# The last z tile inside attention's first steps: its product split over steps 1, 3, 4 and 5, its reciprocal in eight pieces

## The chip, the cores and the metric

The kernel runs on one core of one Trainium2 chip. The metric is the device time of one execution in microseconds (us), and a kernel's time is the median of several executions.

## The reference

One encoder layer on 1024 tokens of width 1024, in float32. What matters here is the middle of it:

```
u = x @ w_in                                   # -> q | k | v | z | x_ssd | B | C | dt
att_out = softmax(q k^T / 8) v                 # 8 query heads of 64, 2 key/value heads, all 1024 keys
y = ssd(...)                                   # two chunked scans, forward and backward
y = y * silu(z)                                # z: 1024 x 512, silu(z) = z / (1 + exp(-z))
mix = concat(att_out, rms(y) * ssd_norm) @ w_out
```

Ahead of it and behind it stand a SwiGLU block, and at the end a gated embedding, each with a layer norm.

## The kernel before

All large products are made from float32 values that are split in two parts each (a rounded high part and the rest, the low part), so that one product of a 128-row block takes three matmuls: high by low, low by high, high by high (`mm3`, L116 to L122). `lo` (L87) is the VectorE subtraction that makes a low part.

The program runs in stages: first SwiGLU; the z tiles; the q, k, v and convolution products; attention; the scans with the first half of `w_out` between them; the second SwiGLU; the gate. z is computed in eight tiles of 128 tokens. Tiles 0 to 5 are made in `z_part`, tile 6 at the end of `xbc_part`, and tile 7 in `z_last` (L1036), which attention calls.

Attention (L1133) is one loop of 72 steps. There are 16 units (two halves of the queries, four pairs of heads, two heads) of four query tiles each, so 64 query tiles. Step i does, in this order:

- `scores(i)`: four matmuls (L1159) into one of two double PSUM tiles named `big`;
- `turn(i - 2)`: eight 128x128 transposes (L1181) of the probabilities of query tile i - 2, into two PSUM tiles named `sm`, and for each a ScalarE cast (L1183), the high part;
- `values`: from step 6 on, four matmuls (L1196, L1197) with v, a quarter of a unit's sum, which fills one `sm` tile over four steps; after the fourth, L1203 (ScalarE) and L1204 (VectorE) take it out, and after every second unit a small reciprocal `rinv` (L1207);
- `normalise`: every eight steps four transposes (L1218) and a VectorE product (L1219);
- `softmax(i)`: a VectorE maximum over the scores (L1166), then a ScalarE exponential (L1168);
- `begin()` in step 1 alone;
- the two VectorE low parts (L87) of `turn`'s tiles;
- in every even step from 8 on, one entry of the list `aside`.

The pool `sm` has four PSUM tiles, each one bank. Which of them an instruction gets, and the order of the instructions on VectorE, ScalarE, GpSimd and the DMA queue, is set by a scheduler when the program is built. TensorE's instructions keep the written order (`in_order`, L1892). An entry of `aside` is put on VectorE and ScalarE behind what the step has issued there (`behind`, L82).

`begin` (in `run`, L1578) calls `z_last`, issues the loads of four 512 KB blocks of `w_out`, and fills `aside`: first z's seven entries, then four that prepare tables for the scans, then eight that split the `w_out` blocks (a ScalarE cast L108, a GpSimd subtraction L87). z's entries are: add 1 to exp(-z) on GpSimd (L1046), the reciprocal of it on VectorE in four pieces of 128 columns (L1049), and the product with z on GpSimd with its store (L1052, L1053). The store is read in the last stage of the scans (L1411).

Of the kernel before, what the change touches and what calls it, by code (L numbers as in the profile page):

```python
# [12 lines left out]
AF = mybir.ActivationFunctionType  # L13
# [5 lines left out]
P = 128  # L19
S = 1024  # L20
D = 1024
NT = S // P
KD = D // P
# [13 lines left out]
class Layer:  # L37
# [998 lines left out]
    def z_last(self, xT, aside):  # L1036

        nc, V = self.nc, self.nc.vector
        ps = self.z_product(NT - 1, xT)
        r = self.ring.tile([P, 1024], F32, name="blk")  # L1040
        z, e = r[:, :512], r[:, 512:]
        V.tensor_copy(z, ps)
        nc.scalar.activation(out=e, in_=ps, func=AF.Exp, scale=-1.0)

        def one_more():
            nc.gpsimd.tensor_scalar(out=e, in0=e, scalar1=1.0, scalar2=None, op0=ALU.add)  # L1046

        def invert(m):
            V.reciprocal(e[:, m], e[:, m])  # L1049

        def silu():
            nc.gpsimd.tensor_tensor(out=z, in0=z, in1=e, op=ALU.mult)  # L1052
            nc.sync.dma_start(out=self.zd[NT - 1], in_=z)  # L1053
        aside += [one_more, *(lambda m=slice(i * P, (i + 1) * P): invert(m) for i in range(4)), silu]


    def ssd_prep(self, wk):
# [75 lines left out]
    def attention(self, c, mixT, aside, begin):  # L1133

        nc, tc = self.nc, self.tc
        Q, K, V = self.qkv
# [6 lines left out]
        def scores(i):  # L1143
            qh, hp, hh = units[i // 4]
            qt, h = i % 4, hp * 2 + hh
            if qt == 0:
                if hh == 0:
                    st[qh, hp] = dict(
                        raw=ev.tile([P, 512], F32, name="a_raw", bufs=2),
                        rsum=self.small.tile([P, 2, 4], F32, name="rsum"))  # L1150

                st[qh, hp, hh] = [[p.tile([P, 4, 512], F32R, name=n) for n in names] for p, names in (
                    ((pt_pool, ("pth0", "pth1")), (pt_pool, ("ptl0", "ptl1"))),
                    ((self.xp, ("xh01", "xl01")), (self.xp, ("xh11", "xl11"))))[hh]]
            q0 = qh * 512 + qt * P
            ps = self.psb()
            for n in range(2):
                for j in range(2):
                    nc.tensor.matmul(ps[:, n * 512:(n + 1) * 512], lhsT=Q[:, h, q0:q0 + P], rhs=K[:, h // 4, j, n * 512:(n + 1) * 512], start=j == 0, stop=j == 1)  # L1159
            return ps  # L1160

        def softmax(i, ps):
            qh, hp, hh = units[i // 4]
            qt = i % 4
            nm = self.small.tile([P, 1], F32, name="nm")
            nc.vector.tensor_reduce(out=nm, in_=ps, axis=AX.X, op=ALU.max, negate=True)  # L1166
            pr = pp.tile([P, S], F32, name="pr")
            nc.scalar.activation(out=pr, in_=ps, func=AF.Exp, bias=nm, scale=1.0, accum_out=st[qh, hp]["rsum"][:, hh, qt:qt + 1])  # L1168
            st[i] = pr

        def turn(i):
            qh, hp, hh = units[i // 4]
            qt = i % 4
            pth, ptl = st[qh, hp, hh]
            pr = st.pop(i)
            los = []
            for half in range(2):
                pt = self.pss().rearrange("p (k t) -> p k t", t=P)
                for k in range(4):
                    kk = half * 4 + k  # L1180
                    nc.tensor.transpose(out=pt[:, k], in_=pr[:, kk * P:(kk + 1) * P], identity=self.ident)  # L1181
                hi, lo = (x[half][:, :, qt * P:(qt + 1) * P] for x in (pth, ptl))
                nc.scalar.copy(out=hi, in_=pt)  # L1183
                los.append((lo, pt, hi))
            return los

        def values(u, part):
            qh, hp, hh = units[u]
            g = (hp * 2 + hh) // 4
            pth, ptl = st[qh, hp, hh]  # L1190
            if part == 0:
                st["po"] = self.pss()
            po = st["po"]
            for k in (2 * part, 2 * part + 1):
                vw = V[:, k, g].rearrange("p a d -> p (a d)")
                nc.tensor.matmul(po, lhsT=vw, rhs=pth[k // 4][:, k % 4], start=k == 0, stop=False)  # L1196
                nc.tensor.matmul(po, lhsT=vw, rhs=ptl[k // 4][:, k % 4], start=False, stop=k == KD - 1)  # L1197
            if part < 3:
                return
            del st[qh, hp, hh]  # L1200
            raw, rsum = st[qh, hp]["raw"], st[qh, hp]["rsum"]
            mine, other = (slice(j * 64, (j + 1) * 64) for j in (hh, 1 - hh))
            nc.scalar.copy(out=raw[mine], in_=po[other])  # L1203
            nc.vector.tensor_tensor(out=raw[mine], in0=po[mine], in1=raw[mine], op=ALU.add)  # L1204
            if hh:
                rinv = self.small.tile([P, 2, 4], F32, name="rinv")
                nc.vector.reciprocal(rinv, rsum)  # L1207
                rx = ev.tile([P, 4, 2, 64], F32, name="rx")
                nc.gpsimd.tensor_copy(rx, rinv.rearrange("p h q -> p q h").unsqueeze(3).broadcast_to([P, 4, 2, 64]))
                st["norm"] = (qh, hp, rx, raw)  # L1210

        def normalise():
            if "norm" not in st:
                return
            qh, hp, rx, raw = st.pop("norm")
            R = self.pss()
            for qt in range(4):
                nc.tensor.transpose(out=R[:, qt * P:(qt + 1) * P], in_=rx[:, qt].rearrange("p h d -> p (h d)"), identity=self.ident)  # L1218
            nc.vector.tensor_tensor(out=raw, in0=raw, in1=R, op=ALU.mult)  # L1219
            hi, lo = (x[:, hp] for x in mixT[qh][0])  # L1220
            nc.gpsimd.tensor_copy(hi, raw)
            nc.gpsimd.tensor_tensor(out=lo, in0=raw, in1=hi.bitcast(F32), op=ALU.subtract)

        n = 4 * len(units)
        for i in range(n + 8):
            ps = scores(i) if i < n else None
            los = turn(i - 2) if 2 <= i < n + 2 else []
            if 6 <= i < n + 6:
                values((i - 6) // 4, (i - 6) % 4)
            if (i - 6) % 4 == 1:  # L1230
                normalise()
            if ps is not None:
                softmax(i, ps)
            if i == 1:
                begin()
            for a in los:
                self.lo(*a)
            if i >= 8 and i % 2 == 0 and aside:
                with self.behind(mybir.EngineType.Activation), self.behind(mybir.EngineType.DVE):
                    aside.pop(0)()  # L1240
# [292 lines left out]
    def run(self):  # L1533
        nc, tc, I = self.nc, self.tc, self.I
        stop = I.get("_stop", 99)
# [35 lines left out]
        with ExitStack() as c:  # L1571
            self.in_proj(c, xT)
            rctx.close()
            with self.behind(mybir.EngineType.SP):
                tabs = self.ssd_tables(tables)
            blocks0, aside = [], []

            def begin():  # L1578
                self.z_last(xT, aside)
                early = [self.ring_raw(I["wm"][k]) for k in range(4)]  # L1580
                aside.extend(tabs)
                aside.extend(lambda i=i, r=r: blocks0.append(self.split(r[:, i * 512:(i + 1) * 512], eng=nc.gpsimd)) for i in range(2) for r in early)

            mixT = [[self.unit(h, 0)] for h in range(2)]
            with ExitStack() as c2:
                self.attention(c2, mixT, aside, begin)
# [27 lines left out]
        late = sctx.enter_context(tc.tile_pool(name="slate", bufs=2))  # L1614
# [80 lines left out]
        with ExitStack() as xc:  # L1695
# [3 lines left out]
            V = nc.vector  # L1699
# [182 lines left out]
        with ExitStack() as c:  # L1882
            rctx.close()
            acc, xT, wg, tp, turn = self.ffn_y(c, 2, lambda t: y2[t], hS, I["wo2"], wT, [I["wg"][0, k] for k in range(4)], xln=1)
# [98 lines left out]
```

## Time and profile before

| | |
|---|---|
| median of 3 runs | 1947.11 us (1946.96 to 1948.23) |
| the profiled execution: its own time | 1948.74 us |
| the profiled execution: span of the trace | 1946.9 us |
| TensorE clock granted | 0.998 of full speed |
| attention's first score load | 878.37 us into the span |
| first matmul of the scans behind it | 1065.27 us |

The span is the time from the first to the last instruction in the trace. The profile names each instruction by its line, its engine, its operation and the tiles that it writes and reads; PE is TensorE's matmuls, PEld TensorE's weight loads, DVE is VectorE, ACT is ScalarE, POOL is GpSimd. In a row of the timeline the first number is the start in us from the span's start, the second the duration, and brackets at the end tell how long the engine sat idle before it and which instruction ended that. A matmul's end is modelled, so the starts of the weight loads, which stand beside every matmul, show TensorE's pace best.

### The profile page before, as it was taken

The page shows a single profiled execution, that of the slowest core. Times are in us where ns is not written, and L with a number is a line of the kernel's source. Part 1 is how long each engine was busy: PE and PEld are TensorE (multiplying, and loading weights), DVE is VectorE, ACT ScalarE, POOL GpSimd, SP SyncE. Part 2 cuts the span into 40 slices and gives each one's busy share as a digit, 9 for nine tenths or more (in the row PEclk, how much of TensorE's full clock was granted, in tenths as well). Part 3 has the DMA queues.
Part 4 walks back from the last instruction along what each step waited for, and adds up shares of the span by engine and source line. Part 5 has one row for each costly group of instructions (what it writes and reads, how often), then busy time and mean ns, then how long its engine had stood idle before and what let it go on. Part 6 is the DMA issues. An engine that isn't in the chain of part 4 may idle for free.

```text
span 1946.9 us, 25645 instructions
## 1 busy us (share of the span) xinstructions
PE 1927.9 (99%) x9132; PEld 1607.8 (83%) x9132; DVE 1528.0 (78%) x2356; ACT 881.1 (45%) x1509; POOL 416.9 (21%) x310
## 2 busy tenths in 40 slices
PE   8999999999999999999999999999999999999998
PEld 6888888888888889888888888888888888888886
DVE  7977777767678668758998878997787787877698
ACT  6433333325444224537887876633333333443311
POOL 0144535430001032001221001013444440001011
PEclk9999999999999999999999999999999999999999
DMA  8434554549866111231002663244545439976022
GB/s 296 143 125 151 190 179 156 190 159 373 297 221 212 63 42 50 84 119 68 7 1 77 212 222 121 90 165 156 190 163 178 173 121 358 331 262 226 32 77 97
DMA packets 147713, 310.34 MB, mean 159 GB/s; under 512 B 18128, under 2 KB 30800, under 8 KB 147584
## 3 DMA queue, kind: packets, MB, share of 16 engines
q1 hardware_dynamic: 147584, 308.69, 45.4%
q8 instruction: 72, 1.18, 0.2%
q14 instruction: 57, 0.47, 0.1%
HBM read 217.21 MB, written 91.42 MB: 159 GB/s over the span
## 4 chain that ended last, share of the span: by engine, by line
PE 94%; DVE 3%; DMA 1%; ACT 1%; issue 1%; POOL 0%; SPq 0%; DVEq 0%; ACTq 0%
PE sm L122 59%; PE big L516 12%; PE sm L516 9%; PE big L122 3%; PE big L1159 3%; PE sm L1181 2%; PE sm L1196 1%; PE sm L1197 1%; DMA yd<-y 1%; DVE nm L1166 1%; DVE conv L977 1%; PE sm L1270 0%; PE big L224 0%; PE sm L224 0%; PE big L909 0%
## 5 line engine op out<-in xcount | busy, mean ns | idle before, releaser
L122 PE MATMUL sm<-xh,blk 128*128 128x512 f32 x1424 | 439.8, 389 | 0.0
L122 PEld LDWEIGHTS sm<-xh,blk 128*128 128x128 f32 x1424 | 267.3, 188 | 55.4
L122 PE MATMUL sm<-xl,blk 128*128 128x512 f32 x736 | 283.8, 389 | 0.0
L122 PE MATMUL sm<-blk,xl 128*128 128x512 f32 (+2 forms) x784 | 238.2, 371 | 0.2 <-ACT xn_t L1010 0.2
L122 PE MATMUL sm<-blk,xh 128*128 128x512 f32 (+2 forms) x584 | 203.3, 379 | 1.6 <-DVE acc L1466 1.1
L108 ACT CAST blk<-raw 128x512 fp32r<-128x512 f32 (+1 forms) x168 | 101.3, 611 | 215.0 <-PE sm L122 134.1
L87 DVE TENSOR_TENSOR blk<-s,blk 128x512 fp32r<-128x512 f32 x176 | 150.8, 861 | 35.2 <-ACT blk L108 33.2
L87 DVE TENSOR_TENSOR blk<-raw,blk 128x512 fp32r<-128x512 f32 (+1 forms) x168 | 146.5, 875 | 40.6 <-ACT blk L108 40.1
L108 ACT CAST blk<-s 128x512 fp32r<-128x512 f32 x172 | 105.7, 622 | 146.5 <-PE sm L122 118.3
L122 PEld LDWEIGHTS sm<-blk,xl 128*128 128x128 f32 x784 | 142.8, 188 | 24.2 <-ACT xn_t L1010 0.5
L122 PEld LDWEIGHTS sm<-xl,blk 128*128 128x128 f32 x736 | 138.2, 188 | 28.6
L178 POOL TENSOR_TENSOR ln_k<-ln_k,mhalf 128x1 f32<-128x1 f32 x32 | 37.4, 1173 | 579.2 <-DVE ln_k L177 563.0
L516 PE MATMUL big<-xh 128*128 128x512 f32 x576 | 138.8, 390 | 0.0
L267 POOL TENSOR_TENSOR s<-raw 128x512 f32<-128x512 f32 x34 | 55.0, 1617 | 387.2 <-DVE blk L87 381.7
L87 DVE TENSOR_TENSOR xh<-blk,xh 128x1024 fp32r<-128x1024 f32 x78 | 95.4, 1223 | 48.4 <-ACT xh L462 42.3
L462 ACT CAST xl<-blk 128x1024 fp32r<-128x1024 f32 x76 | 80.2, 1055 | 113.5 <-PE sm L516 43.7
L462 ACT CAST xh<-blk 128x1024 fp32r<-128x1024 f32 x78 | 82.3, 1055 | 108.1 <-PE big L516 49.9
L122 PEld LDWEIGHTS sm<-blk,xh 128*128 128x128 f32 x584 | 109.9, 188 | 21.3 <-DVE acc L1466 1.4
L516 PEld LDWEIGHTS big<-xh 128*128 128x128 f32 x576 | 107.8, 188 | 22.2
L87 DVE TENSOR_TENSOR xl<-blk,xl 128x1024 fp32r<-128x1024 f32 x76 | 92.7, 1220 | 41.3 <-ACT xl L462 36.7
L516 PE MATMUL big<-xl 128*128 128x512 f32 x480 | 115.8, 390 | 0.0
L122 PE MATMUL sm<-xET2h,blk 128*128 128x512 f32 x352 | 108.4, 389 | 0.0
(343 smaller groups left out, 4018.5 us busy)
## 6 DMA issues: line engine op xcount, KB each, us to landing
raw<-in_wi_dram SPq DMA_DIRECT2D x81, 512.0 KB
blk<-hS SPq DMA_DIRECT2D x154, 256.0 KB
hS<-h SPq DMA_DIRECT2D x88, 256.0 KB
wr<-in_wo_dram SPq DMA_DIRECT2D x44, 512.0 KB
blk<-wT SPq DMA_DIRECT2D x88, 256.0 KB
hS<-sg SPq DMA_DIRECT2D x66, 256.0 KB
wT<-wr SPq DMA_DIRECT2D x66, 256.0 KB
blk<-in_wo_dram SPq DMA_DIRECT2D x66, 256.0 KB
```

Source lines behind the costliest of these rows:

```text
L87: (eng or self.nc.vector).tensor_tensor(out=out, in0=full, in1=hi.bitcast(F32), op=ALU.subtract)
L108: self.nc.scalar.copy(out=b[:, 0, :n], in_=src)
L122: self.nc.tensor.matmul(ps, lhsT=a, rhs=b, start=(i == 0), stop=(i == n - 1))
L178: nc.gpsimd.tensor_tensor(out=r, in0=v, in1=self.mhalf[:, :1], op=ALU.pow)
L267: lambda: G.tensor_tensor(out=s1, in0=a21, in1=a22, op=ALU.add),
L462: A.copy(out=b[:, :, 0], in_=r)
L516: nc.tensor.matmul(ps[q], lhsT=b[:, 0, x, cut], rhs=b[:, 1, y], start=j == i == 0, stop=j == NP - 1 and i == 2)
L977: nc.vector.scalar_tensor_tensor(out=a[:, o], in0=ps[:, o.start + d - c:o.stop + d - c], scalar=cw[:, j, tap:tap + 1], in1=a[:, o], op0=AL ...
L1159: nc.tensor.matmul(ps[:, n * 512:(n + 1) * 512], lhsT=Q[:, h, q0:q0 + P], rhs=K[:, h // 4, j, n * 512:(n + 1) * 512], start=j == 0, stop=j ...
L1166: nc.vector.tensor_reduce(out=nm, in_=ps, axis=AX.X, op=ALU.max, negate=True)
L1181: nc.tensor.transpose(out=pt[:, k], in_=pr[:, kk * P:(kk + 1) * P], identity=self.ident)
L1196: nc.tensor.matmul(po, lhsT=vw, rhs=pth[k // 4][:, k % 4], start=k == 0, stop=False)
```

## The change

`z_last` no longer makes the whole product of tile 7 in step 1. The 24 matmuls of its eight input blocks are cut into four parts: five blocks (15 matmuls) in step 1, and one block (3 matmuls) in each of the steps 3, 4 and 5, behind that step's softmax. The copy out of PSUM and the exponential follow the last part, in step 5. The reciprocal is made of eight entries of 64 columns in `aside` in place of four of 128, so all entries behind the reciprocals move by four entries, which is eight steps. `attention` gets the three late parts from `begin`.

```diff
     def z_last(self, xT, aside):
 
         nc, V = self.nc, self.nc.vector
-        ps = self.z_product(NT - 1, xT)
+        ps = self.pss()
+        pairs = [(x, (w[:, 0], w[:, 1])) for x, w in zip(self.tok(xT, NT - 1), self.wz)]
+
+        def part(ks):
+            for k in ks:
+                (xh, xl), (wh, wl) = pairs[k]
+                for i, (x, w) in enumerate(((xh, wl), (xl, wh), (xh, wh))):
+                    nc.tensor.matmul(ps, lhsT=x, rhs=w, start=k == i == 0, stop=k == KD - 1 and i == 2)
+        part(range(KD - 3))
         r = self.ring.tile([P, 1024], F32, name="blk")
         z, e = r[:, :512], r[:, 512:]
-        V.tensor_copy(z, ps)
-        nc.scalar.activation(out=e, in_=ps, func=AF.Exp, scale=-1.0)
+
+        def end():
+            part((KD - 1,))
+            V.tensor_copy(z, ps)
+            nc.scalar.activation(out=e, in_=ps, func=AF.Exp, scale=-1.0)
...
-        aside += [one_more, *(lambda m=slice(i * P, (i + 1) * P): invert(m) for i in range(4)), silu]
+        aside += [one_more, *(lambda m=slice(i * 64, (i + 1) * 64): invert(m) for i in range(8)), silu]
+        return [lambda: part((KD - 3,)), lambda: part((KD - 2,)), end]
...
             if i == 1:
-                begin()
+                late = begin()
+            if 3 <= i < 6:
+                late.pop(0)()
```

On TensorE the program read before, from the end of z's product (L122, blocks `blk`) on: L1159 are the scores, L1181 the transposes of the probabilities `pr`.

```order
L122 MATMUL sm<-blk,xh_5609 128x512
L122 MATMUL sm<-blk,xl_5608 128x512
L1159 MATMUL big<-K,Q 128x512 x4
L1181 MATMUL sm<-ident,pr 128x128 x8
L1159 MATMUL big<-K,Q 128x512 x4
L1181 MATMUL sm<-ident,pr 128x128 x8
```

Now it reads there, where z's product is L1046, the scores L1171 and the transposes L1193:

```order
L1046 MATMUL sm<-blk,xl_5608 128x512
L1171 MATMUL big<-K,Q 128x512 x4
L1193 MATMUL sm<-ident,pr 128x128 x8
L1171 MATMUL big<-K,Q 128x512 x4
L1193 MATMUL sm<-ident,pr 128x128 x8
L1046 MATMUL sm<-blk,xl_5608 128x512
L1046 MATMUL sm<-blk,xh_5609 128x512
L1046 MATMUL sm<-blk,xl_5608 128x512
L1171 MATMUL big<-K,Q 128x512 x4
L1193 MATMUL sm<-ident,pr 128x128 x8
```

Nine of z's matmuls moved from step 1 behind the transposes of steps 3, 4 and 5; the first such group is shown.

On VectorE, at the first reciprocals (steps 10 to 12), the program read before (L1166 is the maximum, L1204 the addition behind a unit's last values, L87 the low parts, L1049 z's reciprocal):

```order
L1166 TENSOR_REDUCE nm<-big 128x1
L1204 TENSOR_TENSOR a_raw<-sm,a_raw 64x512
L87 TENSOR_TENSOR ptl_7793<-sm,pth_7791 128x4x128
L87 TENSOR_TENSOR ptl_7794<-sm,pth_7792 128x4x128
L1049 RECIPROCAL blk<-blk 128x128
L1166 TENSOR_REDUCE nm<-big 128x1
```

Now, at the same place (the maximum is L1178, the addition L1216, the reciprocal L1060):

```order
L1178 TENSOR_REDUCE nm<-big 128x1
L1216 TENSOR_TENSOR a_raw<-sm,a_raw 64x512
L87 TENSOR_TENSOR ptl_7793<-sm,pth_7791 128x4x128
L87 TENSOR_TENSOR ptl_7794<-sm,pth_7792 128x4x128
L1060 RECIPROCAL blk<-blk 128x64
L1178 TENSOR_REDUCE nm<-big 128x1
```

The pieces keep their places in the even steps 10, 12, 14 and 16 at half the width, and four more stand in steps 18 to 24. z's copy out of PSUM stood between the maxima of steps 1 and 2; it now stands in step 5, between that step's two low parts:

```order
L1178 TENSOR_REDUCE nm<-big 128x1
L87 TENSOR_TENSOR ptl_7582<-sm,pth_7580 128x4x128
L1053 COPY blk<-sm 128x512
L87 TENSOR_TENSOR ptl_7583<-sm,pth_7581 128x4x128
L1178 TENSOR_REDUCE nm<-big 128x1
```

On ScalarE the exponential of z moved likewise, from ahead of step 2's casts to between the two casts of step 6. On the DMA queue the two loads of the scans' first tables (L1292) stood ahead of the four `w_out` loads (L434) and now stand among and behind them. Behind attention, all engines' rows are the same as before.

More of the change, by code (lines that the diff above doesn't have):

```diff
@@ L1578, in begin @@
             def begin():
-                self.z_last(xT, aside)
+                late = self.z_last(xT, aside)
                 early = [self.ring_raw(I["wm"][k]) for k in range(4)]
@@ L1582, in begin @@
                 aside.extend(lambda i=i, r=r: blocks0.append(self.split(r[:, i * 512:(i + 1) * 512], eng=nc.gpsimd)) for i in range(2) for r in early)
+                return late
             mixT = [[self.unit(h, 0)] for h in range(2)]
```

## The prediction

> **What bounds the kernel now.** I read the page first, then attention's stage step by step, because the change touches nothing else.
>
> ```profile
> PE 1927.9 (99%) x9132; PEld 1607.8 (83%) x9132; DVE 1528.0 (78%) x2356; ACT 881.1 (45%) x1509; POOL 416.9 (21%) x310
> ```
>
> TensorE is busy nearly throughout, so the whole kernel can gain only what TensorE waits inside the stage. These are the step's stretches (TensorE's first score load of a step to that of the next): z's product in step 1, then steps 2, 3, 4, 5 and 6, and last a step with values that waits for nothing. The first column is the length, then busy time by engine.
>
> ```profile
> 880.21:885.69 5.48, 5.48 (x25) 4.50 (x24) 1.86 (x2) 3.58 (x5) 0.00 (x0) 1.00 0.78 274
> 885.69:887.60 1.91, 1.91 (x14) 1.65 (x12) 1.26 (x2) 0.68 (x2) 0.00 (x0) 1.00 0.94 296
> 887.60:889.75 2.15, 2.08 (x16) 1.61 (x14) 2.15 (x4) 2.15 (x5) 1.50 (x1) 1.00 0.58 234
> 889.75:891.94 2.19, 2.07 (x13) 1.60 (x13) 2.19 (x4) 2.17 (x5) 0.00 (x0) 1.00 0.00 0
> 891.94:894.26 2.32, 2.08 (x12) 1.60 (x12) 2.32 (x4) 2.16 (x5) 0.00 (x0) 1.00 0.00 0
> 894.26:896.88 2.62, 2.62 (x15) 2.25 (x16) 2.62 (x4) 2.46 (x5) 0.00 (x0) 1.00 0.01 3
> 902.30:905.01 2.71, 2.71 (x18) 2.33 (x17) 2.56 (x5) 2.19 (x5) 0.61 (x1) 1.00 0.00 0
> ```
>
> A step without values costs TensorE 1.91 (step 2), one with values 2.71. Steps 3 to 5 have no values yet took 2.15 to 2.32, and there VectorE (third engine column) is busy to the last. The weight loads show what TensorE waited for, and VectorE's maxima show the pace that was set:
>
> ```profile
> 889.75 0.76 PEld L1159 LDWEIGHTS big<-K,Q 128*128 128x128 f32 x4 [0.30 <-ACT pr L1168]
> 891.94 0.77 PEld L1159 LDWEIGHTS big<-K,Q 128*128 128x128 f32 x4 [0.36 <-ACT pr L1168]
> 894.26 0.77 PEld L1159 LDWEIGHTS big<-K,Q 128*128 128x128 f32 x4 [0.48 <-ACT pr L1168]
> ```
>
> ```profile
> 886.17 0.69 DVE L1042 COPY blk<-sm 128x512 f32<-128x512 f32 x1 [4.10 <-issue]
> 887.03 1.23 DVE L1166 TENSOR_REDUCE nm<-big 128x1 f32<-128x1024 f32 x1 [0.17 <-PE big L1159]
> 891.70 1.21 DVE L1166 TENSOR_REDUCE nm<-big 128x1 f32<-128x1024 f32 x1
> 894.03 1.21 DVE L1166 TENSOR_REDUCE nm<-big 128x1 f32<-128x1024 f32 x1
> ```
>
> Scores wait for a `big` tile that the exponential two steps back must free, and that runs at VectorE's pace: 894.03 - 891.70 = 2.33 for a maximum and two low parts. TensorE catches up with this deficit only once values make its step longer.
>
> The second loss is at the reciprocals. Eight steps each, from step 8, step 16, step 24 and step 40:
>
> ```profile
> 899.60:922.44 22.84, 22.69 (x133) 19.10 (x132) 22.31 (x31) 19.01 (x35) 0.61 (x1) 1.00 0.00 1
> 922.44:945.53 23.09, 22.92 (x134) 18.94 (x133) 22.60 (x31) 19.24 (x35) 3.78 (x4) 1.00 0.03 12
> 945.53:967.78 22.25, 22.25 (x134) 19.02 (x133) 21.12 (x29) 19.87 (x37) 5.01 (x5) 1.00 0.00 1
> 990.04:1012.29 22.25, 22.25 (x134) 19.01 (x133) 21.12 (x29) 19.70 (x37) 5.04 (x5) 1.00 0.00 1
> ```
>
> Later groups take 22.25 with TensorE busy all the time; the two with the four wide reciprocals in them take 22.84 and 23.09, so 0.59 + 0.84 = 1.43 longer. TensorE's waits there name VectorE's low parts:
>
> ```profile
> 915.92 0.88 PEld L1159 LDWEIGHTS big<-K,Q 128*128 128x128 f32 x4
> ...
> 918.78 0.88 PEld L1159 LDWEIGHTS big<-K,Q 128*128 128x128 f32 x4
> ...
> 920.69 0.42 PEld L1181 LDWEIGHTS sm<-ident,pr 128*128 128x128 f32 x4 [0.39 <-DVE xh L87]
> ...
> 923.81 0.42 PEld L1181 LDWEIGHTS sm<-ident,pr 128*128 128x128 f32 x4 [0.61 <-DVE xh L87]
> 924.41 0.42 PEld L1181 LDWEIGHTS sm<-ident,pr 128*128 128x128 f32 x4 [0.18 <-DVE xl L87]
> ...
> 930.53 0.19 PEld L1196 LDWEIGHTS sm<-xh,V 128*128 128x128 f32 x1 [0.18 <-DVE xl L87]
> ```
>
> **The split product.** 24 matmuls took 5.48, so 0.228 each. Nine leave step 1: step 2 starts 2.05 earlier, at 883.64. Each of steps 3, 4 and 5 gets three, 0.68, and costs TensorE 1.91 + 0.68 = 2.59. That is more than VectorE's 2.33, so TensorE no longer waits there: step 3 at 885.55, 4 at 888.14, 5 at 890.73, 6 at 893.32, and step 10 four steps of 2.71 later, 904.16. It was 905.01 (the end of the last stretch above), so the gain is at most 0.85. Equally: the 19.32 from step 2 to step 10 less TensorE's own 4 x 1.91 + 4 x 2.71 = 18.48 leaves 0.84 of waiting.
>
> Three things can cost a part of it. Step 2's scores need the exponential of step 0:
>
> ```profile
> 883.32 0.19 ACT L1168 ACTIVATION_READ_ACCUMULATOR pr<-big,nm 128x1 f32 x1
> ...
> 886.90 0.60 ACT L1043 ACTIVATE blk<-sm 128x512 f32<-128x512 f32 x1 [2.29 <-DVE blk L1042]
> ```
>
> That ends at 883.51, 0.13 ahead. z keeps one `sm` bank up to step 6, so the transposes have three: the second set of each step waits for the first low part of the step before. In step 3 that set is due at 885.55 + 1.4 = 886.95; the maximum of step 2 starts 1.34 behind its scores (887.03 - 885.69), at 884.98, and the low part is done 1.8 later, 886.8. It just fits; in steps 4 and 5 the room is larger by 0.26 each. z's copy (its slot is about 0.6) now delays step 5's second low part, whose bank the first values of step 6 take: maximum of step 5 near 892.0, low part and copy behind it, second low part done near 895.0, values due at 895.1. z's exponential (0.60) sits between step 6's casts and ends near 896.2; the bank that it frees is wanted at 896.9. None of these is a wait by my sum, but three margins near 0.1 make me take 0.7 of the 0.85, with 0 and 0.85 as ends.
>
> **The eight pieces.** VectorE's slots, start to start, in the group that loses most:
>
> ```profile
> 918.69 1.22 DVE L1166 TENSOR_REDUCE nm<-big 128x1 f32<-128x1024 f32 x1
> ...
> 924.27 0.68 DVE L1219 TENSOR_TENSOR a_raw<-a_raw,sm 128x512 f32<-128x512 f32 x1
> 924.87 1.22 DVE L1166 TENSOR_REDUCE nm<-big 128x1 f32<-128x1024 f32 x1
> 926.00 0.19 DVE L1207 RECIPROCAL rinv<-rsum 128x8 f32<-128x8 f32 x1
> 926.11 0.64 DVE L87 TENSOR_TENSOR xh<-sm,xh 128x512 fp32r<-128x512 f32 x1
> 926.67 0.68 DVE L87 TENSOR_TENSOR xl<-sm,xl 128x512 fp32r<-128x512 f32 x1
> 927.27 0.94 DVE L1049 RECIPROCAL blk<-blk 128x128 f32<-128x128 f32 x1
> 928.13 1.16 DVE L1166 TENSOR_REDUCE nm<-big 128x1 f32<-128x1024 f32 x1
> 929.20 0.68 DVE L87 TENSOR_TENSOR xh<-sm,xh 128x512 fp32r<-128x512 f32 x1
> 929.79 0.68 DVE L87 TENSOR_TENSOR xl<-sm,xl 128x512 fp32r<-128x512 f32 x1
> 930.39 0.67 DVE L1204 TENSOR_TENSOR a_raw<-sm,a_raw 64x512 f32<-64x512 f32 x1
> 930.99 1.20 DVE L1166 TENSOR_REDUCE nm<-big 128x1 f32<-128x1024 f32 x1
> ```
>
> A 128-column reciprocal takes 928.13 - 927.27 = 0.86, an 8-column one 0.11, L1219 and L1204 0.60 each. No row shows 64 columns: between 0.11 and 0.86, and on the line through both 0.11 + 56 x 0.75 / 120 = 0.46, which I take. A fixed cost is thus about 0.06 and the four extra pieces add 0.2 of VectorE time in all.
>
> What counts is how they lie. Today, from step 10 to step 18 (nine steps, 22.25 + 2.72 = 24.97 for TensorE), VectorE has 9 x 2.33 + 4 x 0.86 + three L1204 + one L1219 + 0.11 = 26.9: it falls 1.9 behind, and 1.43 of that came out as TensorE's waits. After the change, over the sixteen steps 10 to 25 (44.5): 37.28 + 8 x 0.46 + five L1204 (3.0) + two L1219 (1.2) + two rinv (0.22) = 45.4, so 0.9 behind at the end, and by going through step by step never over 1.1. How much lag is forgiven? The maximum at 918.69, of step 14, is 1.4 late (step 14's scores start at 915.92, and 1.34 later, at 917.26, it was due), and the second set of transposes of step 15 waited 0.39 behind it: so a lag near 1.0 is free, as the three banks give TensorE that much room. The waits of 1.43 should shrink to about 0.15; the ends are 0 and, with 0.86 for a piece, the rival below.
>
> VectorE: DVE Perf Modes in the Trainium skill, under its rules for kernel authors, asks to minimize the number of VectorE operations, which speaks against eight pieces. Its fixed 58 cycles at 0.96 GHz for an operation on SBUF would, as an estimate, make the four extra pieces cost 0.24, beside the 0.2 of the rows; the lag would change by 0.04 and the sum by nothing.
>
> **What else moves.** The entries behind the reciprocals come eight steps later: z's product and its store in step 26, the `w_out` splits (one ScalarE cast, one GpSimd subtraction each) in steps 36 to 50 in place of 28 to 42. The group from 945.53 holds such casts today and takes 22.25, the same as the group from 990.04, so they cost nothing where they go, and 13 steps remain behind the last. z's store is not read before the scans' last stage. The two table loads on the DMA queue, now behind `w_out` loads, have until the scans at 1065. All of that I put at zero.
>
> **The sum.** 0.7 + 1.43 - 0.15 = 2.0 off the profiled span of 1946.9, so 1944.9. That execution took 1948.74 against a median of 1947.11, but the three runs scatter by 1.3 themselves; I take the 2.0 off the median: 1945.1. About 0.2%, 3.9 us, is what a measurement of this kernel can tell from no change, so this is a gain that hardly shows.
>
> **The rivals.**
>
> - *The bank wait takes the place of the early wait.* z's bank is held over five steps, and the second set of transposes waits in steps 3 to 6. For it: margins of 0.1. Against it: attention's later steps run at 2.71 with one of the four banks in use by values. The Trainium skill's Perfetto Trace Analysis, in its optimization strategy, says that repeated gaps can mean too little PSUM. The early gain is then 0: 1947.11 - 1.28 = 1945.8. Chance 0.11.
> - *Slower: a narrow piece costs nearly what a wide one does.* Place: VectorE in steps 10 to 25. At 0.86 a piece VectorE has 41.7 + 6.9 = 48.6 against 44.5, so 4.1 behind, 1.0 forgiven: 3.1 of waits in place of 1.43, and with the early 0.7 kept a loss of 1.0: 1948.1. It decides from 0.74 a piece on: 41.7 + 8 x 0.74 - 44.5 - 1.0 = 2.1, today's 1.43 and the early 0.7. Against it: 0.11 for eight columns leaves little fixed cost. Chance 0.05.
> - *The 2.0 are won and lost again,* at a transfer behind attention that doesn't start earlier: 1947.1. Against it: what follows is issued behind attention's own work. Chance 0.07.
>
> My forecast has 0.70. All four lie within 3.9 us of the time before, 0.93 together; I leave 0.04 for faster and 0.03 for slower by more than that, for what none of them covers. The range: all 2.3 of waiting gone and the scatter of 0.9 below gives 1943.9; nothing gained and a little scatter 1947.4. The slower rival (0.05) and what none covers (0.07) are left out of it.
>
> **What would show it.** In the profile after: from attention's first score load to step 10 about 0.7 shorter; weight loads of steps 3 to 5 without waits for the exponential; the eight-step groups from steps 8 and 16 near 22.3 and 22.4, with VectorE busy almost throughout as far as step 25; a reciprocal of 64 columns with a slot of 0.46. Wrong it would be if transposes in steps 3 to 6 wait for low parts by 0.3 or more each, if a piece takes over 0.6, or if the stretch from 1065 on grows by what attention lost.

## The result

| | before | after |
|---|---|---|
| median of all runs | 1948.25 us (22 runs) | 1945.20 us (22 runs) |
| ratio after / before | | 0.9986, 95% interval 0.998 to 0.9991 |
| span of the profiled execution | 1946.9 us | 1943.3 us |
| attention: TensorE's first score matmul to the first matmul of the scans | 878.59 to 1065.27: 186.68 us | 877.81 to 1062.17: 184.36 us |
| first score matmul to step 10's first score load | 26.42 us | 25.40 us |
| eight steps from step 8, from step 16, from step 24 | 22.84, 23.09, 22.25 us | 22.32, 22.26, 22.30 us |

The forecast was 1945.1, with a gain of 2.0. Attention became 2.32 shorter, and the ratio says 2.7 (1.8 to 3.9) for the whole: faster, by no more than the 0.2% that was set as the bound. That 1945.20 stands so near to 1945.1 is luck in part: the 2.0 were taken off the 1947.11 of three runs, and the median of the 22 runs before is 1948.25. A median over many executions holds some that ran undisturbed and a few that did not; the ratio uses the undisturbed ones alone.

The profile after, first the page's line of busy times, then the steps' stretches, cut at the first score load of each step as in the prediction: the first scores with z's five blocks, step 2, the three filled steps, step 6, step 7.

```profile
PE 1925.4 (99%) x9132; PEld 1607.5 (83%) x9132; DVE 1521.2 (78%) x2360; ACT 880.8 (45%) x1509; POOL 416.9 (21%) x310
```

```profile
877.59:882.88 5.29, 5.29 (x25) 4.32 (x24) 2.35 (x2) 3.40 (x6) 1.43 (x2) 1.00 0.82 264
882.88:884.78 1.90, 1.90 (x13) 1.65 (x12) 0.56 (x1) 1.02 (x3) 0.00 (x0) 1.00 0.97 291
884.78:887.17 2.39, 2.39 (x17) 2.07 (x16) 2.39 (x4) 2.39 (x5) 0.00 (x0) 1.00 0.94 382
887.17:889.65 2.48, 2.48 (x17) 2.14 (x15) 2.48 (x4) 2.45 (x6) 0.00 (x0) 1.00 0.03 12
889.65:892.14 2.49, 2.49 (x17) 2.14 (x16) 2.49 (x4) 2.29 (x5) 0.00 (x0) 1.00 0.00 0
892.14:895.09 2.95, 2.95 (x18) 2.35 (x16) 2.95 (x5) 2.75 (x6) 0.00 (x0) 1.00 0.01 3
895.09:897.80 2.71, 2.71 (x18) 2.33 (x17) 2.71 (x5) 2.50 (x5) 1.50 (x1) 1.00 0.00 0
```

Steps 3 to 5 now have TensorE busy to the last, at 2.39 to 2.49, with three more matmuls in each; before, they took 2.15 to 2.32 with waits in them. Step 6 has one wait that was not there: 2.95 where a step with values takes 2.71. TensorE's weight loads show it at the first values, and VectorE's rows what it waited for:

```profile
882.88 0.87 PEld L1171 LDWEIGHTS big<-K,Q 128*128 128x128 f32 x4
883.79 1.02 PEld L1193 LDWEIGHTS sm<-ident,pr 128*128 128x128 f32 x8
884.78 0.77 PEld L1171 LDWEIGHTS big<-K,Q 128*128 128x128 f32 x4
885.60 1.03 PEld L1193 LDWEIGHTS sm<-ident,pr 128*128 128x128 f32 x8
...
893.06 1.03 PEld L1193 LDWEIGHTS sm<-ident,pr 128*128 128x128 f32 x8
894.29 0.19 PEld L1208 LDWEIGHTS sm<-pth,V 128*128 128x128 f32 x1 [0.20 <-issue]
```

```profile
892.34 0.68 DVE L87 TENSOR_TENSOR ptl<-sm,pth 128x512 fp32r<-128x512 f32 x1
892.94 0.68 DVE L1053 COPY blk<-sm 128x512 f32<-128x512 f32 x1
893.54 0.68 DVE L87 TENSOR_TENSOR ptl<-sm,pth 128x512 fp32r<-128x512 f32 x1
...
924.27 0.54 DVE L1060 RECIPROCAL blk<-blk 128x64 f32<-128x64 f32 x1
924.73 1.16 DVE L1178 TENSOR_REDUCE nm<-big 128x1 f32<-128x1024 f32 x1
```

z's copy (892.94) pushes step 5's second low part to 893.54; it ends at 894.22, and the first values load at 894.29. The row of that load names no releaser; that the values wait for the bank that this low part frees is a reading, and the run with the copy behind it tests it. A narrow reciprocal's slot is 924.73 - 924.27 = 0.46. The eight-step groups, of which the third holds the last narrow piece and the fourth none:

```profile
897.80:920.12 22.32, 22.32 (x133) 19.09 (x132) 21.46 (x31) 19.02 (x35) 0.61 (x1) 1.00 0.00 1
920.12:942.38 22.26, 22.26 (x135) 19.02 (x134) 22.17 (x33) 18.85 (x34) 2.48 (x3) 1.00 0.00 1
942.38:964.68 22.30, 22.30 (x134) 19.00 (x133) 21.72 (x31) 19.05 (x35) 3.74 (x4) 1.00 0.03 12
964.68:986.93 22.25, 22.25 (x134) 19.01 (x133) 21.12 (x29) 19.86 (x37) 5.03 (x5) 1.00 0.00 1
```

VectorE is busy for 22.17 of 22.26 in the second: nearly all its slack is used, and TensorE hardly waits.

### The profile page after: what moved, and what is told of

The parts are those of the page before. It is cut to its first block, busy times and chain, and to the rows that moved or that the text cites. A ratio compares the mean times of both kernels' runs of the same rounds, so it can differ in the third digit from the quotient of the medians.

```text
span 1943.3 us, 25645 instructions
## 1 busy us (share of the span) xinstructions
PE 1925.4 (99%) x9132; PEld 1607.5 (83%) x9132; DVE 1521.2 (78%) x2360; ACT 880.8 (45%) x1509; POOL 416.9 (21%) x310
## 4 chain that ended last, share of the span: by engine, by line
PE 96%; DVE 2%; DMA 1%; ACT 1%; issue 0%; POOL 0%; SPq 0%; DVEq 0%; ACTq 0%
PE sm L122 58%; PE big L516 12%; PE sm L516 9%; PE big L1171 3%; PE sm L1193 3%; PE big L122 3%; PE sm L1208 1%; PE sm L1209 1%; PE sm L1385 1%; DVE conv L977 1%; PE sm L1284 0%; PE sm L1295 0%; PE big L909 0%; PE big L224 0%; PE big L1700 0%; PE sm L224 0%
## 5 line engine op out<-in xcount | busy, mean ns | idle before, releaser
L122 PE MATMUL sm<-xh,blk 128*128 128x512 f32 x1424 | 439.6, 389 | 0.0
L122 PEld LDWEIGHTS sm<-xh,blk 128*128 128x128 f32 x1424 | 267.3, 188 | 55.3
L122 PE MATMUL sm<-xl,blk 128*128 128x512 f32 x736 | 283.8, 389 | 0.0
L122 PE MATMUL sm<-blk,xl 128*128 128x512 f32 (+2 forms) x768 | 233.2, 371 | 0.2 <-ACT xn_t L1010 0.2
L122 PE MATMUL sm<-blk,xh 128*128 128x512 f32 (+2 forms) x576 | 200.2, 379 | 1.3 <-DVE acc L1480 0.8
L87 DVE TENSOR_TENSOR blk<-s,blk 128x512 fp32r<-128x512 f32 x176 | 150.1, 857 | 39.6 <-ACT blk L108 37.8
L87 DVE TENSOR_TENSOR blk<-raw,blk 128x512 fp32r<-128x512 f32 (+1 forms) x168 | 143.0, 855 | 39.5 <-ACT blk L108 38.9
L122 PEld LDWEIGHTS sm<-xl,blk 128*128 128x128 f32 x736 | 138.2, 188 | 28.7
L122 PEld LDWEIGHTS sm<-blk,xl 128*128 128x128 f32 x768 | 139.9, 188 | 23.6 <-ACT xn_t L1010 0.5
L87 DVE TENSOR_TENSOR xh<-blk,xh 128x1024 fp32r<-128x1024 f32 x78 | 95.2, 1220 | 49.2 <-ACT xh L462 44.7
L122 PEld LDWEIGHTS sm<-blk,xh 128*128 128x128 f32 x576 | 108.3, 188 | 20.6 <-DVE acc L1480 1.1
L87 DVE TENSOR_TENSOR xl<-blk,xl 128x1024 fp32r<-128x1024 f32 x76 | 92.7, 1219 | 41.2 <-ACT xl L462 36.6
L122 PE MATMUL sm<-xET2h,blk 128*128 128x512 f32 x352 | 108.3, 389 | 0.0
```

Source lines behind the costliest of these rows:

```text
L87: (eng or self.nc.vector).tensor_tensor(out=out, in0=full, in1=hi.bitcast(F32), op=ALU.subtract)
L122: self.nc.tensor.matmul(ps, lhsT=a, rhs=b, start=(i == 0), stop=(i == n - 1))
```

## The experiments

All were run with the kernel before on the same chip. Attention's length is taken from each kernel's own profile, as above. Where a ratio's interval holds 1, the whole execution shows no difference, and what follows rests on attention's length in one profile.

| | attention | to step 10 | groups from step 8, 16, 24 | median | ratio to before (95%) |
|---|---|---|---|---|---|
| before | 186.68 | 26.42 | 22.84, 23.09, 22.25 | | |
| after | 184.36 | 25.40 | 22.32, 22.26, 22.30 | 1945.20 | 0.9986 (0.998 to 0.9991) |
| before once more | 186.68 | 26.42 | 22.84, 23.10, 22.25 | 1947.68 | 0.9996 (0.9988 to 1.0005) |
| split product alone | 185.66 | 25.39 | 22.85, 23.09, 22.26 | 1947.14 | 0.9994 (0.9986 to 1.0003) |
| eight pieces alone | 185.35 | 26.40 | 22.32, 22.26, 22.31 | 1946.28 | 0.9991 (0.9983 to 1.0) |
| four wide, spread | 185.06 | 25.39 | 22.32, 22.64, 22.64 | 1946.89 | 0.999 (0.9981 to 0.9999) |
| eight narrow, two at once | 185.74 | 25.42 | 22.87, 23.13, 22.25 | 1947.07 | 0.9993 (0.9985 to 1.0002) |
| narrow pieces made twice | 187.49 | 25.41 | 22.86, 24.06, 23.10 | 1948.37 | 1.0 (0.9991 to 1.0009) |
| bank held, nothing to fill | 186.44 | 27.46 | 22.35, 22.25, 22.32 | 1947.88 | 0.9996 (0.9988 to 1.0005) |
| copy behind the low parts | 184.14 | 25.18 | 22.32, 22.25, 22.32 | 1945.38 | 0.9985 (0.9976 to 0.9993) |
| four wide, far apart | 184.31 | 25.42 | 22.33, 22.25, 22.25 | 1945.47 | 0.9985 (0.9976 to 0.9994) |
| wide far apart, and copy behind | 184.08 | 25.18 | 22.32, 22.25, 22.26 | 1945.21 | 0.9985 (0.9976 to 0.9994) |

The theory was the prediction's: TensorE's waits in attention are VectorE's pace in steps 3 to 5, and VectorE's lag behind the bunched reciprocals. The rivals were that the held bank takes the early gain back, and that it is the pieces' size, or the rest of the program, that gives the gain.

**Before once more.** No edit.

> The kernel before, unchanged, profiled once more. Between the two profiles attention (TensorE's first score matmul to the first matmul of the scans) went from 186.68 us to 184.36 us, 2.32 less, but the span fell by 3.6: 0.78 of that ahead of attention's start (878.59 to 877.81) and 0.5 behind it. Theory: the 1.3 outside attention is scatter between executions. Then attention here is 186.7 within 0.1, while its start and the tail behind it differ from the first profile by some tenths up to 1 us. Rival: the outside part belongs to the change. Then start and tail repeat, 878.6 and 881.6, within 0.1.

Attention repeated to the hundredth, 186.68. Its start was at 878.61, but the tail behind it took 880.8 us against 881.6 in the first profile. Over all the profiles taken here (before, after, and ten experiments) the start lies between 877.60 and 878.84 and the tail between 880.3 and 881.6, in no relation to the edit. The 1.3 us by which after's one profile was shorter outside attention is of this size, so it is not the change's. Within attention, differences of 0.1 us can be read from single profiles: beside this one repeat, the eight steps from step 32, which no edit touches, take 22.25 in all twelve. Of whole executions only the ratios can be compared.

**The split product alone.**

```diff
-        aside += [one_more, *(lambda m=slice(i * 64, (i + 1) * 64): invert(m) for i in range(8)), silu]
+        aside += [one_more, *(lambda m=slice(i * P, (i + 1) * P): invert(m) for i in range(4)), silu]
```

> The split product alone, the reciprocal in four wide pieces as before. Theory: the two parts act apart. First score load to that of step 10 takes 25.6 us (26.6 before), the two eight-step groups with the reciprocals stay near 22.8 and 23.1, attention 185.7. Rival, the early gain is eaten by VectorE: TensorE comes earlier to the wide reciprocals with VectorE as late as before, so their waits grow by what was gained, attention near 186.5.

```profile
898.28:921.13 22.85, 22.70 (x134) 19.10 (x133) 22.00 (x30) 18.80 (x35) 0.61 (x1) 1.00 0.00 1
921.13:944.22 23.09, 22.92 (x135) 18.94 (x134) 22.60 (x31) 19.22 (x35) 3.78 (x4) 1.00 0.03 12
```

The early stretch has the whole gain of 1.02, and the two groups are those of before: 185.66, as the theory said. The early gain is not eaten later.

**The eight pieces alone.** The kernel before with the opposite of that edit.

> The eight narrow pieces alone, z's product whole in step 1 as before. Theory: groups 22.3 and 22.3, the early stretch 26.6 as before, attention 185.3. Rival, the gain at the reciprocals came from TensorE's other arrival: groups over 22.6, attention over 185.8. With the run before it, the two gains should add to 2.3 within 0.2.

```profile
898.58:920.90 22.32, 22.32 (x133) 19.09 (x132) 21.81 (x32) 19.24 (x35) 0.61 (x1) 1.00 0.00 1
920.90:943.16 22.26, 22.26 (x135) 19.02 (x134) 22.17 (x33) 18.84 (x34) 2.48 (x3) 1.00 0.01 1
```

185.35: 1.33 less than before. With 1.02 from the other part the sum is 2.35; both together gave 2.32. The two parts act apart.

**Four wide pieces over the same sixteen steps.** In after:

```diff
-        aside += [one_more, *(lambda m=slice(i * 64, (i + 1) * 64): invert(m) for i in range(8)), silu]
+        aside += [one_more, *(f for i in range(4) for f in (lambda m=slice(i * P, (i + 1) * P): invert(m), lambda: None)), silu]
```

> As after, but the reciprocal in four pieces of 128 columns, in steps 10, 14, 18 and 22 (an empty entry of the list behind each). Theory, that it is the spread over sixteen steps that counts: VectorE has even less to do (4 x 0.86 in place of 8 x 0.46), groups of 22.3 to 22.4, attention 184.3 to 184.6. Rival, that the size of a single piece counts: a wide piece makes VectorE 0.86 late at once, the transposes behind it wait each time, groups 22.6 and more, attention 185 and more.

```profile
920.40:943.04 22.64, 22.64 (x134) 18.93 (x133) 22.35 (x31) 19.03 (x34) 2.92 (x4) 1.00 0.00 1
943.04:965.68 22.64, 22.63 (x134) 18.92 (x133) 21.74 (x30) 19.05 (x35) 3.34 (x4) 1.00 0.03 12
```

```profile
921.61 0.42 PEld L1193 LDWEIGHTS sm<-ident,pr 128*128 128x128 f32 x4 [0.44 <-DVE xh L87]
922.21 0.42 PEld L1193 LDWEIGHTS sm<-ident,pr 128*128 128x128 f32 x4 [0.18 <-DVE xl L87]
944.25 0.42 PEld L1193 LDWEIGHTS sm<-ident,pr 128*128 128x128 f32 x4 [0.45 <-DVE xh L87]
944.85 0.42 PEld L1193 LDWEIGHTS sm<-ident,pr 128*128 128x128 f32 x4 [0.18 <-DVE xl L87]
```

185.06, between the two: spreading alone gives 0.60 of the 1.30 that after has over the split product alone (185.66 to 184.36). So spread was not the whole of it, although VectorE had less work than in after. But the waits are not behind each wide piece. They stand in steps 16 and 24 alone, right behind the four transposes of `normalise` in steps 15 and 23, which take a third bank until VectorE's product has read it. There even the first transposes of a step wait for the low part of the step just before; the wide pieces of steps 14 and 22 come just ahead, those of steps 10 and 18 show no wait behind them. Two things meet in those steps. VectorE's lag, counted as in the prediction, is larger: 1.33 in step 15 (scores at 917.13, maximum at 919.80) against 1.07 in step 11 (906.21 and 908.62). And less of it is forgiven: in after a lag of 1.02 in step 23 made step 24 take 2.68 in place of the 2.61 that it takes with wide pieces far apart (below), while the 1.07 here made step 12 no longer. How much of the 0.70 that this run loses against after belongs to each was not separated.

**Eight narrow pieces, two at a time.** In after:

```diff
-        aside += [one_more, *(lambda m=slice(i * 64, (i + 1) * 64): invert(m) for i in range(8)), silu]
+        aside += [one_more, *(lambda ms=[slice(j * 64, (j + 1) * 64) for j in (2 * i, 2 * i + 1)]: [invert(m) for m in ms] for i in range(4)), silu]
```

> As after, but the eight narrow pieces go two at a time into steps 10, 12, 14 and 16, where the wide ones were. Theory (spread counts): VectorE's work there is 0.2 more than with wide pieces, so the groups are 22.9 and 23.1, attention 185.7 to 185.9. Rival (narrow pieces as such help, because something else gets between them): groups near 22.4, attention 184.5.

```profile
898.75:921.62 22.87, 22.72 (x134) 19.11 (x133) 21.99 (x33) 18.80 (x35) 0.61 (x1) 1.00 0.00 1
921.62:944.75 23.13, 22.93 (x135) 18.93 (x134) 22.64 (x32) 19.21 (x35) 3.78 (x4) 1.00 0.03 12
```

185.74, 0.08 more than with the wide pieces in the same four steps. Narrow pieces gain nothing by being narrow. Nothing gets in between them: the two of step 10 start at 908.44 and 908.89.

**Narrow pieces made twice.** In after, with `spare` a scratch tile of 64 columns:

```diff
             V.reciprocal(e[:, m], e[:, m])
+            V.reciprocal(self.spare, e[:, m])
```

> As after, but each narrow reciprocal is made twice, the second time into a scratch tile that nobody reads, so a piece takes 0.92 us or a little more of VectorE. Theory, by the prediction's account of VectorE's time: 41.7 + 8 x 0.92 = 49.1 against TensorE's 44.5 in steps 10 to 25, 4.6 behind, 1.0 forgiven, 3.6 of waits: attention 187.9, slower than before by 1.2. Rival, TensorE's room is larger than 1.0 or VectorE catches up elsewhere: attention under 186.5.

```profile
898.16:921.02 22.86, 22.71 (x134) 19.11 (x133) 21.98 (x32) 18.92 (x35) 0.61 (x1) 1.00 0.00 1
921.02:945.08 24.06, 23.51 (x135) 18.94 (x134) 23.97 (x37) 19.01 (x34) 2.50 (x3) 1.00 0.00 1
945.08:968.18 23.10, 22.91 (x135) 18.96 (x133) 22.61 (x33) 19.23 (x35) 3.74 (x4) 1.00 0.03 12
```

187.49, 0.81 longer than before: the slower rival's mechanism is real; what it had wrong is the price of one narrow piece. The three groups hold 0.61 + 1.81 + 0.85 = 3.27 us over 3 x 22.25, where 3.6 was worked out; the account of VectorE's time holds within a tenth. For the whole execution the ratio of 1.0 cannot show 0.8 us.

**The bank held with nothing to fill it.** z's product whole in step 1, its copy left in step 5, ahead of both low parts there (the exponential follows as in after):

```diff
-        part(range(KD - 3))
+        part(range(KD))
...
-            part((KD - 1,))
-            V.tensor_copy(z, ps)
+            with self.behind(mybir.EngineType.DVE):
+                V.tensor_copy(z, ps)
...
-        return [lambda: part((KD - 3,)), lambda: part((KD - 2,)), end]
+        return [lambda: None, lambda: None, end]
```

> z's product whole in step 1 as before, but its copy and exponential stay in step 5, so that z's PSUM bank is held over the same steps as after while TensorE gets nothing to fill them with; narrow pieces. Theory: the bank costs next to nothing by itself; first score load to that of step 10 takes 26.6 to 26.9, attention 185.3 to 185.6. Rival, the held bank makes the transposes wait: waits for low parts in steps 3 to 6, 27.2 and more, attention 186 and more.

TensorE's weight loads in its step 6, and VectorE's rows of step 5, which fall into the same time:

```profile
895.91 0.42 PEld L1193 LDWEIGHTS sm<-ident,pr 128*128 128x128 f32 x4 [0.83 <-DVE ptl L87]
896.51 0.19 PEld L1208 LDWEIGHTS sm<-pth,V 128*128 128x128 f32 x1 [0.18 <-DVE ptl L87]
```

```profile
893.45 1.21 DVE L1178 TENSOR_REDUCE nm<-big 128x1 f32<-128x1024 f32 x1
894.58 0.68 DVE L1053 COPY blk<-sm 128x512 f32<-128x512 f32 x1
895.18 1.27 DVE L87 TENSOR_TENSOR ptl<-sm,pth 128x512 fp32r<-128x512 f32 x2
896.37 1.21 DVE L1178 TENSOR_REDUCE nm<-big 128x1 f32<-128x1024 f32 x1
```

The theory missed here: 27.46 to step 10, 1.06 more than with the pieces alone, 1.02 of it in step 6 (3.63 against 2.61). Steps 3 to 5 cost nothing more, at 2.15, 2.19 and 2.32. In step 6 the second transposes wait 0.83 for a low part that stands behind the copy. Before, the copy lay in step 2, where VectorE waited anyway (its row showed 4.10 idle ahead of it); in step 5 VectorE sets the pace, and the copy's 0.60 (894.58 to 895.18) counts in full. That the bank, three for the transposes in place of four, lets TensorE feel it at once is argued: how much of the 1.06 is the copy's place and how much the bank's was not separated. By these rows, as an estimate, the low part would be done 0.60 earlier without the copy ahead of it, and about 0.2 of the 0.83 would be left. So the bank rival had a mechanism, dearer than I had it. In after, where the filled steps give VectorE 2.48 for its 2.33, only the 0.24 in step 6 came, and the next run takes that away too with the bank still held.

**The copy behind both low parts.** In after:

```diff
-            if 3 <= i < 6:
-                late.pop(0)()
+            last = 3 <= i < 6 and late.pop(0)()
             for a in los:
                 self.lo(*a)
+            if last:
+                with self.behind(mybir.EngineType.DVE):
+                    last()
```

where the third late part returns the copy and the exponential as a function in place of issuing them.

> As after, but z's copy out of PSUM comes behind both low parts of step 5, not between them. After showed one wait left in the early steps: step 6 took 2.95 in place of 2.71, its first values waiting for the second low part, which the copy had delayed. Theory: with the copy behind, step 6 takes 2.71, attention 184.1. Rival: the wait moves on, to the transposes of step 7, which need z's bank (the exponential now comes later): attention 184.4 as after or longer.

```profile
893.16 0.88 PEld L1174 LDWEIGHTS big<-K,Q 128*128 128x128 f32 x4
894.09 1.03 PEld L1196 LDWEIGHTS sm<-ident,pr 128*128 128x128 f32 x8
895.08 0.19 PEld L1211 LDWEIGHTS sm<-pth,V 128*128 128x128 f32 x1
...
895.89 0.88 PEld L1174 LDWEIGHTS big<-K,Q 128*128 128x128 f32 x4
```

The values load without a wait, step 6 takes 895.89 - 893.16 = 2.73, and step 7 takes 2.72. Attention is 0.22 shorter, 184.14: the wait came from the copy's place ahead of the low part, and it did not move on.

**Four wide pieces far apart,** from the reading of the spread wide pieces. In after, three empty entries between the pieces, so that all entries behind them come ten steps later than in after:

```diff
-        aside += [one_more, *(lambda m=slice(i * 64, (i + 1) * 64): invert(m) for i in range(8)), silu]
+        aside += [one_more, *(f for i in range(4) for f in (lambda m=slice(i * P, (i + 1) * P): invert(m), *[lambda: None] * (3 if i < 3 else 0))), silu]
```

> As after, but four wide pieces in steps 10, 18, 26 and 34. With wide pieces in steps 10, 14, 18 and 22 the waits stood only in steps 16 and 24, behind the four transposes of L1230 in steps 15 and 23, which hold one PSUM bank until VectorE's product has read it; none stood behind the pieces of steps 10 and 18. Theory: a wide piece costs nothing where VectorE has six steps to make up for it before the next such transposes; groups of 22.25 to 22.32, attention 184.2 to 184.4, as with eight narrow pieces. Rival, wide pieces cost where they are: groups 22.4 and more, attention 184.8 and more.

```profile
897.94:920.27 22.33, 22.33 (x134) 19.09 (x133) 21.34 (x29) 19.07 (x36) 0.61 (x1) 1.00 0.00 1
920.27:942.52 22.25, 22.25 (x135) 19.02 (x134) 21.73 (x30) 18.98 (x35) 2.45 (x3) 1.00 0.00 1
```

184.31, 0.05 below after. Wide pieces cost nothing here, where VectorE has five steps between a piece and the next `normalise`.

**Both mended places together.**

> Four wide pieces in steps 10, 18, 26 and 34, and z's copy behind both low parts of step 5: the two mended places together. Theory: step 6 takes 2.72, the groups 22.25 to 22.32, attention 184.0 to 184.15, the shortest of all; the whole execution cannot be told from after, 0.2 to 0.35 us being below its scatter. Rival: the two meet somewhere, attention above 184.2.

184.08, the shortest of all, 0.28 below after; the whole execution (1945.21) cannot be told from after's.

## Why the prediction was right

- **The split product: the mechanism held, the term was too small.** 0.7 was taken and 0.85 called the most; it gave 1.02. The step that failed is TensorE's own cost of a step without values, read as 1.91 from step 2. Rows of z's matmuls in step 3 after, and of the scores behind them, show how the reading went wrong:

```profile
886.60 0.19 PEld L1046 LDWEIGHTS sm<-blk,xl 128*128 128x128 f32 x1
886.71 0.19 PEld L1046 LDWEIGHTS sm<-blk,xh 128*128 128x128 f32 x1
...
887.17 0.39 PE L1046 MATMUL sm<-blk,xl 128*128 128x512 f32 x1
887.17 0.87 PEld L1171 LDWEIGHTS big<-K,Q 128*128 128x128 f32 x4
887.40 1.08 PE L1171 MATMUL big<-K,Q 128*128 128x512 f32 x4
```

The first score load starts together with z's last matmul, 0.23 ahead of its own. So a stretch that is cut at score loads holds the last matmul of the step before, and not its own last one. Step 2 stands behind z's product: its 1.91 holds a matmul of z (0.23) in place of a transpose (0.11, the distance of the first two rows), and a step between transposes costs about 1.79. Steps 3 to 5 took 2.39, 2.48 and 2.49 in place of 2.59, 0.41 less in all; with the 0.85 that makes 1.26 of waiting before, and step 6's wait took 0.24 of it back. The prediction's own rows said as much: the three waits in them, 0.30, 0.36 and 0.48, are 1.14 already.

- **The three margins.** The exponential of step 0 and the transposes of step 3 showed no wait, though 0.1 was all they had by the working. The third, z's copy ahead of a low part that the values need, was put at 0.1 to spare and cost 0.24, by the same mistake: that low part was done 16.63 behind attention's first score load, just as worked out (895.0 - 878.37), but TensorE reached step 6 after 14.55 and not after 14.95.
- **The eight pieces: right in mechanism and size.** A narrow slot was put at 0.46 and is 0.46. The waits were to fall from 1.43 to 0.15; the groups now hold 0.07 + 0.01 + 0.05 = 0.13 over 22.25. The lag was to be never over 1.1, and 0.9 at the end; after shows it largest in step 23 and, behind the last piece, in step 26:

```profile
939.10 0.88 PEld L1171 LDWEIGHTS big<-K,Q 128*128 128x128 f32 x4
941.46 1.16 DVE L1178 TENSOR_REDUCE nm<-big 128x1 f32<-128x1024 f32 x1
...
947.77 0.87 PEld L1171 LDWEIGHTS big<-K,Q 128*128 128x128 f32 x4
950.04 1.21 DVE L1178 TENSOR_REDUCE nm<-big 128x1 f32<-128x1024 f32 x1
```

The maxima come 2.36 and 2.27 behind their scores, 1.02 and 0.93 later than the 1.34 of an undelayed step. The lag account also foretold the doubled pieces to a tenth. What it lacked is that the forgiven lag is not the same in each step: about 1.0 in most, less behind `normalise`. With eight narrow pieces this hardly mattered; four wide ones over the same steps lost 0.70 against them, in part by it.

- **What was put at zero** (the later entries, the loads, the store) cost nothing that shows: the pieces alone, which have all the moves behind them, gave 1.33, all of it at the reciprocals. (z had six entries in `aside` before, not seven: one addition, four pieces, one product. The steps that the prediction names go by six.)
- **The sum.** 2.0 forecast and 2.32 in attention. The difference of the two medians, 3.05, is more than that, and the profiles outside attention scatter by over 1 us with no relation to the edit; before's identical copy also had a median 0.46 below before's own. I read the difference as 2.3, which the ratio's interval (1.8 to 3.9) holds.
- **The rivals.** A wait for a bank came at one place, 0.24. The slower one did not happen, since a narrow piece takes about half of a wide one. Nothing was lost behind attention that shows above the scatter there.

## What to carry to other kernels

A helper engine whose work per step is a little less than the bounding engine's can take extra work for free only as fast as its slack refills it; cut the extra work or spread it so that its lag stays under what the buffers forgive, and look for the steps in which a buffer is taken by something else, for there the least is forgiven. Work of the bounding engine that has no due time belongs into the steps in which that engine waits for others. When a result is moved to a later step, its way out (here a copy) moves with it: look at what stands behind it there.

## What the runs showed of the hardware

- The reciprocal on VectorE goes by columns: slots of 0.11, 0.46 and 0.86 us for 8, 64 and 128 columns of 128 partitions, so about 6.3 ns a column and 0.06 fixed.
- A weight load starts with the matmul ahead of its own: z's last matmul and the first score load both stand at 887.17, the score's matmul at 887.40. So the distance between the first loads of two groups holds one matmul of the group before: four score loads take 0.82 behind transposes (884.78 to 885.60) and 0.91 behind 512-column matmuls (882.88 to 883.79).
- The attention stage of one program, 186.68 us, repeated to 0.01 us between two executions, while over the twelve profiles the 878 us ahead of it and the 881 behind it vary by over 1 us each, in no relation to the edit.
